# A two-layer hybrid encoder on one core: the q/kv projection group made token-major, and layer 1's modulation and conv taps spread anew

## The chip, the core and the metric

The kernel runs on one core of a Trainium2 chip. The core has five engines with a queue each: PE multiplies matrices, DVE (VectorE) and ACT (ScalarE) do elementwise work, POOL (GpSimd) small work, and SP issues DMA transfers. PE writes only to PSUM (eight banks of 128 x 512 f32), from where DVE or ACT fetch the results. The metric is the device time of one execution in microseconds (us).

## The reference

The input x is 256 tokens by 2048 channels, in f32, and goes through two layers. Each layer normalizes x, scales and shifts it by vectors made from c ("modulation"), projects it with one matrix of 4288 columns, runs four mixers on parts of the columns, projects back, and then does a gated feed-forward part with a width-3 convolution.

```python
c_act = silu(c)
for l in range(2):
    mod = (c_act @ w_mod[l] + b_mod[l]).reshape(bn, 6, d)     # shift, scale, gate for mixing, and again for the FFN
    h = layer_norm(x) * (1.0 + scale_m) + shift_m
    uv, q_c, kv_c, k_r, sb, sc, sh, ag = split(h @ w_in[l])   # widths 1024, 384, 256, 64, 512, 512, 512, 1024
    y_a = gmlp_mixer(uv, ...)        # u * (W_s LN(v) + b), W_s masked: rows 64.. see columns 64.. only
    y_b = mla_mixer(q_c, kv_c, k_r, ...)
    y_c = short_conv_mixer(sb, sc, sh, ...)
    y_d = conformer_conv(ag, ...)    # GLU, depthwise causal conv of 31 taps, layer norm, swish
    y = concatenate([y_a, y_b, y_c, y_d]) @ w_out[l]
    x = layer_norm(ALPHA * x + (1.0 + gate_m) * y) * g + b
    h = layer_norm(x) * (1.0 + scale_f) + shift_f
    x = layer_norm(ALPHA * x + (1.0 + gate_f) * conv_ffn(h, ...)) * g + b

def mla_mixer(q_c, kv_c, k_r, ...):
    q = rms_norm(q_c, q_norm_g) @ w_uq      # rms_norm: x * rsqrt(mean(x^2) + eps) * g
    kv = rms_norm(kv_c, kv_norm_g) @ w_ukv
    k_rope = apply_rope(k_r, cos, sin)
    ...                                     # masked softmax attention, 4 heads
```

The change touches the product that gives q_c, kv_c and k_r (704 columns, group "B" below), the rms_norm behind it, the mask of W_s, and the order of some work.

## The kernel before

**Products.** The input projection is cut into groups of columns: D (ag, 1024), U and V (uv, 512 each), B (q_c, kv_c, k_r, loaded 768 wide), C (sc and sh, 1024) and E (sb, 512). Each group runs over 16 k-tiles of 128 rows of w_in. In layer 1 a weight tile (`wraw`, from DRAM) is split into a rounded part `whi` (ACT, L455) and a rest `wlo` (DVE, L456), both in the reduced type fp32r; the activations are split likewise (`hT`), and each product is made as three fp32r products: hi x hi, hi x rest, rest x hi. The split tiles have four buffers each, the raw ones four in all. In layer 0, groups B and C use exact f32 products instead, with no split (`wexact`, `hF`); an exact product appears in the trace as two records.

`group` computes channel-major results: 128 weight columns are the stationary operand, 256 tokens stream by, and six blocks of 128 columns fill three PSUM banks two by two (`B_c`). All matmuls go through `mm`, so they carry line 79.

**Staging.** `run` goes through the units of a group: `stream` loads a unit, then issues the products of the unit before, then `pump()`s the modulation, then takes up to `bg` pieces off the list of background work. Layer 1's groups come in the order V, D, U, B, C, E, then the output projection ("out").

**Modulation.** The products with w_mod are made on DVE: for each k-tile a 1 MB transfer (`wmod`) and one step over 128 x 2048 elements (`macc`, L233 and L235), sixteen steps for each of the six vectors of a layer. How many steps go with one unit of a group is set by `RATES`.

**Taps.** The 31-tap convolution of group D is made of 124 small operations, 31 for each of four channel blocks: the first of a block is on ACT, the other 30 on DVE (L834). They wait on the background list until the units of U, B, C and E take them (`STEPS` says how many a unit takes).

**The order on an engine.** The program is given in the order in which the functions issue it, and a planner then interleaves it by its own estimates: for instance it puts C products between the steps of `mix_b`, and taps wherever it takes DVE to be free. What comes out is fixed when the program is built: each engine runs its own list in order, and an instruction that waits holds all behind it.

**mix_b** (L950 on) takes group B's result. It squares five of the six blocks on ACT (L968), scales q_c by its gain into `qg` (ACT, L972) and kv_c into `kvr` (DVE, L975), and multiplies the rotary key by cosine and sine into `kc` (DVE, L978 and L979). The mean squares need sums over channels, which lie on partitions, so PE sums them with a column of ones (`ps_ss`); DVE scales them and adds epsilon (L987, L990), POOL raises them to -1/2 (L105), and for kv_c a diagonal matrix and a product with ones (`ps_rkv`) bring the factors to all partitions, where DVE multiplies them in (L1003). The factor of q_c is left to the softmax's scale. Then `ps_kr` (the rotary key), `ps_qn`, `ps_qr`, `ps_kn`, `ps_v`, the scores `ps_sc` and so on.

**mix_v** makes the gated mixer. PE transposes the spatial weights (`ps_wT`), DVE copies them to `wT` (L914), and POOL then writes zeros on the masked block (L915); `ps_mix` on PE reads wT.

Of the kernel before, what the change touches and what calls it, by code (L numbers as in the profile page):

```python
# [7 lines left out]
F32 = mybir.dt.float32  # L8
F32R = mybir.dt.float32r
AF = mybir.ActivationFunctionType  # L10
ALU = mybir.AluOpType
AX = mybir.AxisListType

P = 128
D = 2048
S = 256
DEPTH = 2
W_G = 512
KT = D // P
D_FF = 5632  # L20
NF = D_FF // P
Q_LORA = 384
KV_LORA = 256
HEADS = 4
IN_COLS = 4288
C_UV, C_Q, C_SB, C_SC, C_AG = 0, 1024, 1728, 2240, 3264
ALPHA = (2.0 * DEPTH) ** 0.25
LN_EPS = 1e-5
RMS_EPS = 1e-6
ATT_SCALE = 192.0 ** -0.5  # L30
# [3 lines left out]

RATES = [
    dict(B=1.3, C=1.6, out=2.1, up=0.7, down=0.7),
    dict(D=0.2, U=0.4, V=0.0, B=0.2, C=0.5, E=0.6, out=0.6, up=0.3, down=0.7),
]

STEPS = [  # L40
    dict(B=7, C=8, up=2),
    dict(U=6, B=5, C=6, E=6, up=2),
]

PIECES = ((0, 2), (2, 2), (4, 4), (8, 4), (12, 4))
# [5 lines left out]
def encoder_kernel(ctx: ExitStack, tc: tile.TileContext, A: dict, consts: bass.AP, out: bass.AP):  # L51
# [17 lines left out]
    def tmp_tile(name):  # L69
        return tmpp.tile([P, 512], F32, tag="tmp", name=name)  # L70

    def ms_tile(name):
        return msp.tile([P, 512], F32, tag="ms", name=name)

    def acc_tile(name):
        return accp.tile([P, 512], F32, tag="acc", name=name)

    def mm(o, lhsT, rhs, start, stop):
        pe.matmul(o, lhsT, rhs, start=start, stop=stop, skip_group_check=True)  # L79
# [4 lines left out]
    def slot(name, dtype=F32):  # L84
        return slotp.tile([P, 1024], dtype, tag="slot", name=name)
# [14 lines left out]
    pool.memset(ones, 1.0)  # L100
    mhalf = keep.tile([P, 4], F32, name="mhalf")
    pool.memset(mhalf, -0.5)

    def power(o, i):
        pool.tensor_tensor(out=o, in0=i, in1=mhalf[:, : i.shape[1]], op=ALU.pow)  # L105
# [361 lines left out]
    hT = []  # L467
# [60 lines left out]
    def group2(w, c0, name, then, bg=0, spare=0):  # L528
# [21 lines left out]

        return KT // nk, load, products, lambda: then(box["c"]), bg

    hN, first = [], []

    def first_group(w, c0, then):
# [23 lines left out]
    def run(g):  # L579
        units, load, products, end, bg = g  # L580
        for u in range(units):
            stream(lambda: load(u), lambda item, u=u: products(item, u), bg)
        pending.append(end)
# [223 lines left out]
    def mixers(l, w_in, Y, hF=None, between=None):  # L807
# [91 lines left out]
        def mix_v():  # L899
            ua, va = Y["a"], Y["v"]  # L900
            ga = raw_tile("gmlp")
            nc.sync.dma_start(
                out=ga[:, 0:512].rearrange("p (h j) -> p h j", h=4), in_=A["gmlp_w_s"][l].rearrange("h i j -> i h j")
            )
            nc.sync.dma_start(out=ga[:, 512:1024], in_=A["gmlp_ln_g"][l].partition_broadcast(P))
            nc.sync.dma_start(out=ga[:, 1024:1536], in_=A["gmlp_ln_b"][l].partition_broadcast(P))
            nc.sync.dma_start(
                out=ga[:, 1536:2048], in_=A["gmlp_b_s"][l].rearrange("h i -> (h i)").partition_broadcast(P)
            )
            wT = slot("wT")[:, :512].rearrange("p (h i) -> p h i", h=4)  # L910
            ps = ms_tile("ps_wT")
            for h in range(4):
                pe.transpose(ps[:, h * P : (h + 1) * P], ga[:, h * P : (h + 1) * P], ident)
            dve.tensor_copy(wT, ps.rearrange("p (h i) -> p h i", h=4))  # L914
            pool.memset(wT[64:128, :, 0:64], 0.0)  # L915
            for t in range(2):
                st = smallp.tile([P, 1, 6], F32, tag="stA", name="stA")
                dve.bn_stats(out=st[:, 0, :], in_=va[:, t, :])
                mv, r = rstd_of(st, f"A{t}", False)
                dve.scalar_tensor_tensor(  # L920
                    out=va[:, t, :], in0=va[:, t, :], scalar=mv[:, 0:1], in1=ga[:, 512:1024], op0=ALU.subtract, op1=ALU.mult
                )
                dve.scalar_tensor_tensor(
                    out=va[:, t, :], in0=va[:, t, :], scalar=r[:, 0:1], in1=ga[:, 1024:1536], op0=ALU.mult, op1=ALU.add
                )
            for b in range(2):
                ps = ms_tile("ps_mix")
                for hh in range(2):
                    h = 2 * b + hh
                    for t in range(2):  # L930
                        o = ps[:, hh * S + t * P : hh * S + (t + 1) * P]
                        mm(o, va[:, t, h * P : (h + 1) * P], wT[:, h, :], True, True)
                mixed = tmp_tile("mixed").rearrange("p (h t i) -> p h t i", h=2, t=2)
                bias = ga[:, 1536 + b * S : 1536 + (b + 1) * S].rearrange("p (h i) -> p h i", h=2)
                for t in range(2):
                    dve.tensor_tensor(
                        out=mixed[:, :, t, :],
                        in0=ps.rearrange("p (h t i) -> p h t i", h=2, t=2)[:, :, t, :],
                        in1=bias,
                        op=ALU.add,  # L940
                    )
                dve.tensor_tensor(
                    out=ua[:, 2 * b : 2 * b + 2, :],
                    in0=ua[:, 2 * b : 2 * b + 2, :],
                    in1=mixed.rearrange("p h t i -> p h (t i)"),
                    op=ALU.mult,
                )


        def mix_b(cps, _):  # L950
            wq0, wq1, wkv = raw_tile("wq0"), raw_tile("wq1"), raw_tile("wkv")
            WQ = [wq0[:, 0:768], wq0[:, 768:1536], wq1[:, 0:768]]
            for j in range(3):
# [3 lines left out]
            nc.sync.dma_start(  # L957
                out=wkv.rearrange("p (k c) -> p k c", k=2), in_=A["mla_w_ukv"][l].rearrange("(k p) c -> p k c", p=P)
            )
            qg = slot("qg")[:, :768].rearrange("p (j s) -> p j s", j=3)  # L960
            kvr = slot("kvr")[:, :768].rearrange("p (j s) -> p j s", j=3)
            bank = [(cps[i // 2], (i % 2) * S) for i in range(6)]
            sq = [tmp_tile("sqB0"), tmp_tile("sqB1"), tmp_tile("sqB2")]
            sqs = []
            for i in range(5):
                ps, o = bank[i]
                s = sq[i // 2][:, (i % 2) * S : (i % 2) * S + S]
                act.activation(out=s, in_=ps[:, o : o + S], func=AF.Square)  # L968
                sqs.append(s)
            for j in range(3):  # L970
                ps, o = bank[j]
                act.activation(out=qg[:, j, :], in_=ps[:, o : o + S], func=AF.Copy, scale=QG(j))  # L972
            for j in range(2):
                ps, o = bank[3 + j]
                dve.tensor_scalar(out=kvr[:, j, :], in0=ps[:, o : o + S], scalar1=KVG(j), scalar2=None, op0=ALU.mult)  # L975
            ps, o = bank[5]
            kc, ks = tmp_tile("kc"), None
            dve.tensor_tensor(out=kc[0:64, 0:S], in0=ps[0:64, o : o + S], in1=cosT[0:64, :], op=ALU.mult)  # L978
            dve.tensor_tensor(out=kc[0:64, S : 2 * S], in0=ps[0:64, o : o + S], in1=sinT[0:64, :], op=ALU.mult)  # L979
            ps = ms_tile("ps_ss")  # L980
            for t in range(2):
                for j in range(3):
                    mm(ps[:, t : t + 1], sqs[j][:, t * P : (t + 1) * P], ones[:, 0:1], j == 0, j == 2)
                for j in range(2):
                    mm(ps[:, 2 + t : 3 + t], sqs[3 + j][:, t * P : (t + 1) * P], ones[:, 0:1], j == 0, j == 1)
            rr = smallp.tile([P, 8], F32, tag="rr", name="rr")
            dve.tensor_scalar(  # L987
                out=rr[:, 0:2], in0=ps[:, 0:2], scalar1=1.0 / Q_LORA, scalar2=RMS_EPS, op0=ALU.mult, op1=ALU.add
            )
            dve.tensor_scalar(  # L990
                out=rr[:, 2:4], in0=ps[:, 2:4], scalar1=1.0 / KV_LORA, scalar2=RMS_EPS, op0=ALU.mult, op1=ALU.add
            )
            power(rr[:, 4:8], rr[:, 0:4])
            dve.tensor_scalar(out=rr[:, 4:6], in0=rr[:, 4:6], scalar1=ATT_SCALE, scalar2=None, op0=ALU.mult)
            dg = tmp_tile("dgB")
            for t in range(2):
                dve.tensor_scalar(
                    out=dg[:, t * P : (t + 1) * P], in0=ident, scalar1=rr[:, 6 + t : 7 + t], scalar2=None, op0=ALU.mult
                )
            ps = ms_tile("ps_rkv")  # L1000
            mm(ps[:, :S], ones, dg[:, :S], True, True)
            for j in range(2):
                dve.tensor_tensor(out=kvr[:, j, :], in0=kvr[:, j, :], in1=ps[:, :S], op=ALU.mult)  # L1003

            rope = slot("rope").rearrange("p (j s) -> p j s", j=4)
            ps = ms_tile("ps_kr")
# [157 lines left out]
        phase(l, "U")  # L1164
        run(group(w_in, C_UV, 512, f"U{l}", mix_uv, nk=4, bg=STEPS[l]["U"]))
        phase(l, "B")
        run(group(w_in, C_Q, 768, f"B{l}", mix_b, bg=STEPS[l]["B"]))
        phase(l, "C")
        run(group(w_in, C_SC, 1024, f"C{l}", mix_c, bg=STEPS[l]["C"]))
        phase(l, "E")  # L1170
# [3 lines left out]
    def by_pieces(l, w_in, hF, between, mix_d, mix_u, gelu_v, mix_v, mix_b, mix_c, mix_e):  # L1174
# [93 lines left out]
            gelu_v(t, sums["V"][t])  # L1268
        mix_v()
        phase(l, "B")  # L1270
        run(group(w_in, C_Q, 768, f"B{l}", mix_b, hF=hf, bg=STEPS[l]["B"]))
        phase(l, "C")

        def mix_ce(cps, tps):
# [260 lines left out]
```

## Time and profile before

| | us |
|---|---|
| three runs | 2286.57, 2292.60, 2292.98 (median 2292.6) |
| the profiled execution, its own time | 2285.5 |
| its span, first to last instruction | 2283.7 |
| PE busy | 2226.7 (98%) |
| DVE busy | 1788.8 (78%) |
| ACT busy | 1049.8 (46%) |
| POOL busy | 35.3 (2%) |

All lines below come from the profiled execution. A row of the instructions in order of time gives start, length, engine, line, operation, what it writes from what it reads, shapes and count; in brackets stands the engine's idle time before it and what ended that. A row of grouped instructions has busy time and mean length (ns) after the first bar, and the idle time before the group after the second. A row of the chain of waits has start, length, engine, tile and count.

### The profile page before, as it was taken

Reading aid. Unit: us, or ns where it says so; the run is one execution under the profiler, and the core shown is the slowest. Engines: PE = TensorE matmul, PEld = TensorE weight load, DVE = VectorE, ACT = ScalarE, POOL = GpSimd, SP = SyncE. Lnnn points to the kernel's source line nnn. Section 1 sums busy time; section 2 is a strip of 40 time slices with the busy share of each in tenths; the row PEclk is TensorE's granted clock in tenths of the full one; section 3 lists DMA queues with packets and bytes.
Section 4 is the critical chain, followed back from the end, with each engine's and each line's share of the span. In section 5 each row is a group of like instructions: output and inputs, shape, how many; then the busy total and the mean of one; then the engine's idle time right before and its main releaser. Section 6 shows DMA issues by size and latency. Waiting matters only on the chain. (4 is left out here: it accounts for less than half of the span.)

```text
span 2283.7 us, 30024 instructions
## 1 busy us (share of the span) xinstructions
PE 2226.7 (98%) x11682; PEld 1859.8 (81%) x11682; DVE 1788.8 (78%) x2270; ACT 1049.8 (46%) x1525; POOL 35.3 (2%) x59
## 2 busy tenths in 40 slices
PE   5899999999999999999999999999999999999998
PEld 4688886478888888887887999877888888888886
DVE  6878998598888898998976799787776565665676
ACT  2221141355554544544556434556555554454553
POOL 2000000000000000000000000000000000000000
PEclk9999999999999999999999999999999999999999
DMA  9999889778998988888974666876765556555554
GB/s 348 368 335 342 304 301 393 301 267 304 319 329 302 323 312 327 317 316 304 319 258 148 200 214 240 291 268 223 247 223 190 184 182 199 186 196 190 193 194 147
DMA packets 224566, 605.21 MB, mean 265 GB/s; under 512 B 14548, under 2 KB 27076, under 8 KB 202660
## 3 DMA queue, kind: packets, MB, share of 16 engines
q1 hardware_dynamic: 223576, 602.30, 74.7%
q8 instruction: 91, 1.49, 0.3%
q0 software_dynamic: 848, 1.01, 0.1%
q14 instruction: 51, 0.42, 0.0%
HBM read 601.16 MB, written 2.10 MB: 264 GB/s over the span
## 5 line engine op out<-in xcount | busy, mean ns | idle before, releaser
L456 DVE TENSOR_TENSOR wlo<-wraw,whi 128x1024 fp32r<-128x1024 f32 (+1 forms) x624 | 749.6, 1214 | 315.5 <-ACT whi L455 309.4
L455 ACT CAST whi<-wraw 128x1024 fp32r<-128x1024 f32 (+1 forms) x624 | 649.2, 1047 | 727.2 <-PE g_c L79 204.4
L79 PE MATMUL v_c<-hT,whi 128*128 128x512 f32 x1408 | 493.1, 394 | 0.0
L79 PE MATMUL g_c<-hT,whi 128*128 128x512 f32 x1280 | 448.2, 394 | 0.0
L79 PE MATMUL v_c<-hT,wlo 128*128 128x256 f32 x1408 | 394.3, 280 | 0.0
L79 PE MATMUL d<-whi,a 128*128 128x512 f32 x1344 | 387.9, 390 | 0.0
L235 DVE SCALAR_TENSOR_TENSOR macc<-wmod,cact,macc 128x2048 f32<-128x2048 f32 x150 | 351.6, 2344 | 17.1 <-DMA wmod<-in_w_mod_dram 16.8
L79 PE MATMUL g_c<-hT,wlo 128*128 128x256 f32 x1280 | 358.4, 280 | 0.0
L79 PEld LDWEIGHTS v_c<-hT,whi 128*128 128x128 f32 x1408 | 263.9, 187 | 61.0
L79 PEld LDWEIGHTS d<-whi,a 128*128 128x128 f32 x1344 | 252.9, 188 | 52.4
L79 PEld LDWEIGHTS g_c<-hT,whi 128*128 128x128 f32 x1280 | 239.9, 187 | 55.6
L79 PEld LDWEIGHTS v_c<-hT,wlo 128*128 128x128 f32 x1408 | 265.8, 189 | 0.2
L79 PEld LDWEIGHTS g_c<-hT,wlo 128*128 128x128 f32 x1280 | 241.7, 189 | 0.2
L79 PE MATMUL d<-wlo,a 128*128 128x512 f32 x672 | 233.8, 390 | 1.9 <-DVE wlo L456 1.9
L79 PEld LDWEIGHTS d<-wlo,a 128*128 128x128 f32 x672 | 126.6, 188 | 29.1 <-DVE wlo L456 2.7
L79 PE MATMUL o<-whi,a 128*128 128x512 f32 x352 | 102.3, 398 | 2.3 <-ACT whi L455 2.3
L834 DVE SCALAR_TENSOR_TENSOR convD<-gluD,pm,convD 128x237 f32<-128x237 f32 (+26 forms) x240 | 99.0, 458 | 0.5
L474 ACT CAST a<-g 128x512 fp32r<-128x512 f32 x132 | 81.1, 616 | 36.7 <-PE d L79 34.2
L79 PE MATMUL D_c<-hT,whi 128*128 128x256 f32 x448 | 85.7, 292 | 4.0 <-ACT hT L474 3.0
L475 DVE TENSOR_TENSOR a<-g,a 128x512 fp32r<-128x512 f32 x132 | 87.5, 683 | 1.8 <-ACT a L474 1.8
L566 PE MATMUL first<-wexact,hN 128*128 128x512 f32 x192 | 85.7, 596 | 1.5 <-ACT hN L82 1.2
L235 DVE SCALAR_TENSOR_TENSOR qacc<-wmod,cact,qacc 128x1024 f32<-128x1024 f32 (+1 forms) x75 | 80.2, 1070 | 2.4 <-DMA wmod<-in_w_mod_dram 0.4
(311 smaller groups left out, 2462.3 us busy)
## 6 DMA issues: line engine op xcount, KB each, us to landing
wraw<-in_ffn_w_up_dram SPq DMA_DIRECT2D x168, 1024.0 KB, 5.2
wmod<-in_w_mod_dram SPq DMA_DIRECT2D x160, 1024.0 KB, 6.6
wraw<-in_ffn_w_down_dram SPq DMA_DIRECT2D x88, 1024.0 KB, 5.3
wmod<-in_w_mod_dram SPq DMA_DIRECT2D x64, 512.0 KB, 7.9
wraw<-in_w_in_dram SPq DMA_DIRECT2D x30, 1024.0 KB, 5.5
wexact<-in_w_in_dram SPq DMA_DIRECT2D x52, 512.0 KB, 6.7
wraw<-in_w_out_dram SPq DMA_DIRECT2D x24, 1024.0 KB, 7.3
wexact<-in_w_out_dram SPq DMA_DIRECT2D x16, 512.0 KB, 11.0
```

The costliest lines, as they stand in the source:

```text
L79: pe.matmul(o, lhsT, rhs, start=start, stop=stop, skip_group_check=True)
L235: i = dve.scalar_tensor_tensor(out=acc, in0=w, scalar=col, in1=acc, op0=ALU.mult, op1=ALU.add)
L455: held(act.copy(hi[:, :m], r), "cast")
L456: i = dve.tensor_tensor(out=lo[:, :m], in0=r, in1=hi[:, :m].bitcast(F32), op=ALU.subtract)
L474: act.copy(hi, src)
L475: dve.tensor_tensor(out=lo, in0=src, in1=hi.bitcast(F32), op=ALU.subtract)
L566: i = pe.matmul(ps, hN[kt // 4][:, kt % 4, t * P : (t + 1) * P], parts[kt], start=kt == 0, stop=kt == KT - 1, skip_group_check=True,)
L834: dve.scalar_tensor_tensor(out=yd[:, j, 30 - k :], in0=glu[:, j, : S - 30 + k], scalar=CW(k, j), in1=yd[:, j, 30 - k :], op0=ALU.mult, op1 ...
```

## The change

Four edits stand together.

**Group B becomes token-major.** A new `latent_group` takes the place of `group` for B in both layers. The activations of 128 tokens are the stationary operand and the weight columns stream by: for each k-tile, token tile and term one product of 512 columns into a bank of its own (`B_w`) and one of 192 columns into half of a shared bank (`B_n`). 704 columns are loaded in place of 768.

**mix_b works on rows of tokens.** The squares are taken by ACT with an accumulated sum along the row, so PE's sums, the diagonal matrix and the broadcast go; POOL adds the two parts of kv_c's sum, adds epsilon and takes the power, ATT_SCALE being put into the constants. ACT copies q_c and the rotary key, and copies kv_c scaled by its factor; twelve transposes on PE then turn these to channel-major, where gains and cosines are applied as before.

**RATES and STEPS of layer 1.** More modulation steps with D and E's units, none with U's, B's and C's; taps per unit 7, 4, 4 and 8 for U, B, C and E.

**wT.** The zeros are written ahead of the transposes, and DVE copies only the rest, in two pieces.

```diff
 RATES = [
     dict(B=1.3, C=1.6, out=2.1, up=0.7, down=0.7),
-    dict(D=0.2, U=0.4, V=0.0, B=0.2, C=0.5, E=0.6, out=0.6, up=0.3, down=0.7),
+    dict(D=1.0, U=0.0, V=0.0, B=0.0, C=0.0, E=0.9, out=0.6, up=0.3, down=0.7),
 ]
 STEPS = [
     dict(B=7, C=8, up=2),
-    dict(U=6, B=5, C=6, E=6, up=2),
+    dict(U=7, B=4, C=4, E=8, up=2),
 ]
+    rms_eps = keep.tile([P, 4], F32, name="rms_eps")
+    pool.memset(rms_eps[:, 0:2], RMS_EPS / ATT_SCALE**2)
+    pool.memset(rms_eps[:, 2:4], RMS_EPS)
+    def latent_group(w, c0, name, then, hF=None, bg=0):
+        nk = 2
+        box = {}
+        def products(item, u):
+            if u == 0:
+                box["wide"] = [acc_tile(f"{name}_w{t}") for t in range(2)]
+                both = acc_tile(f"{name}_n")
+                box["narrow"] = [both[:, t * 192 : (t + 1) * 192] for t in range(2)]
+                box["h"] = list(hT)
+            for k, (hi, lo) in enumerate(item):
+                kt = u * nk + k
+                st, sp = kt == 0, kt == KT - 1
+                for t in range(2):
+                    tok = slice(t * P, (t + 1) * P)
+                    outs = ((box["wide"][t], slice(0, 512), st), (box["narrow"][t], slice(512, 704), st and t == 0))
+                    if lo is None:
+                        for o, c, first in outs:
+                            mm(o, hF(kt)[:, tok], hi[:, c], first, sp)
+                        continue
+                    xh, xl = (h[:, kt % 2, tok] for h in box["h"][kt // 2][:2])
+                    for o, c, first in outs:
+                        mm(o, xh, hi[:, c], first, False)
+                    for o, c, _ in outs:
+                        mm(o, xh, lo[:, c], False, False)
+                    for o, c, _ in outs:
+                        mm(o, xl, hi[:, c], False, sp)
+        def load(u):
+            return weights(w, u * nk, nk, c0, 704, hF is not None)
+        return KT // nk, load, products, lambda: then(box["wide"], box["narrow"]), bg
...
+            pool.memset(wT[64:128, :, 0:64], 0.0)
             ps = ms_tile("ps_wT")
...
-            dve.tensor_copy(wT, ps.rearrange("p (h i) -> p h i", h=4))
-            pool.memset(wT[64:128, :, 0:64], 0.0)
+            by_head = ps.rearrange("p (h i) -> p h i", h=4)
+            dve.tensor_copy(wT[0:64], by_head[0:64])
+            dve.tensor_copy(wT[64:128, :, 64:128], by_head[64:128, :, 64:128])
...
-        def mix_b(cps, _):
+        def mix_b(wide, narrow):
...
+            lat = [tmp_tile("lat0"), tmp_tile("lat1"), tmp_tile("lat2")]
+            rest = [lat[2][:, t * 192 : (t + 1) * 192] for t in range(2)]
+            ss = smallp.tile([P, 8], F32, tag="rr", name="ss")
+            for t in range(2):
+                for at, junk, ps, n in (
+                    (0, lat[t][:, 0:384], wide[t][:, 0:384], Q_LORA * ATT_SCALE**2),
+                    (2, lat[t][:, 384:512], wide[t][:, 384:512], KV_LORA),
+                    (4, rest[t][:, 0:128], narrow[t][:, 0:128], KV_LORA),
+                ):
+                    act.activation(
+                        out=junk, in_=ps, func=AF.Square, scale=float(n) ** -0.5, accum_out=ss[:, at + t : at + t + 1]
+                    )
+                act.copy(lat[t][:, 0:384], wide[t][:, 0:384])
+                act.copy(rest[t][:, 128:192], narrow[t][:, 128:192])
+            rr = smallp.tile([P, 8], F32, tag="rr", name="rr")
+            pool.tensor_tensor(out=ss[:, 2:4], in0=ss[:, 2:4], in1=ss[:, 4:6], op=ALU.add)
+            pool.tensor_tensor(out=rr[:, 0:4], in0=ss[:, 0:4], in1=rms_eps, op=ALU.add)
+            power(rr[:, 4:8], rr[:, 0:4])
+            for t in range(2):
+                for o, ps in ((lat[t][:, 384:512], wide[t][:, 384:512]), (rest[t][:, 0:128], narrow[t][:, 0:128])):
+                    act.activation(out=o, in_=ps, func=AF.Copy, scale=rr[:, 6 + t : 7 + t])
...
+            def turn(ps, o, parts):
+                for t in range(2):
+                    n = parts[t].shape[1]
+                    pe.transpose(ps[0:n, o + t * P : o + (t + 1) * P], parts[t], ident)
+                return ps[:, o : o + S]
+            ps = ms_tile("ps_q")
+            for j in range(2):
+                by = turn(ps, j * S, [lat[t][:, j * P : (j + 1) * P] for t in range(2)])
+                act.activation(out=qg[:, j, :], in_=by, func=AF.Copy, scale=QG(j))
...
+            ps = ms_tile("ps_kv")
+            for j in range(2):
+                by = turn(ps, j * S, [lat[t][:, 384:512] if j == 0 else rest[t][:, 0:128] for t in range(2)])
+                dve.tensor_scalar(out=kvr[:, j, :], in0=by, scalar1=KVG(j), scalar2=None, op0=ALU.mult)
...
-        run(group(w_in, C_Q, 768, f"B{l}", mix_b, bg=STEPS[l]["B"]))
+        run(latent_group(w_in, C_Q, f"B{l}", mix_b, bg=STEPS[l]["B"]))
...
-        run(group(w_in, C_Q, 768, f"B{l}", mix_b, hF=hf, bg=STEPS[l]["B"]))
+        run(latent_group(w_in, C_Q, f"B{l}", mix_b, hF=hf, bg=STEPS[l]["B"]))
```

More of the change, by code (lines that the diff above doesn't have):

```diff
@@ L960, in mix_b @@
             qg = slot("qg")[:, :768].rearrange("p (j s) -> p j s", j=3)
             kvr = slot("kvr")[:, :768].rearrange("p (j s) -> p j s", j=3)
[L962 to L969, printed above, removed]
@@ L970, in mix_b @@
-            for j in range(3):
-                ps, o = bank[j]
-                act.activation(out=qg[:, j, :], in_=ps[:, o : o + S], func=AF.Copy, scale=QG(j))
-            for j in range(2):
[L974 to L1001, printed above, removed]
+            def turn(ps, o, parts):
[3 more added lines that the diff above has]
+                return ps[:, o : o + S]
@@ new lines, in mix_b @@
+            ps = ms_tile("ps_q")
+            for j in range(2):
+                by = turn(ps, j * S, [lat[t][:, j * P : (j + 1) * P] for t in range(2)])
+                act.activation(out=qg[:, j, :], in_=by, func=AF.Copy, scale=QG(j))
+            ps = ms_tile("ps_q")
+            by = turn(ps, 0, [lat[t][:, 256:384] for t in range(2)])
+            act.activation(out=qg[:, 2, :], in_=by, func=AF.Copy, scale=QG(2))
+            by = turn(ps, S, [rest[t][:, 128:192] for t in range(2)])
+            kc = tmp_tile("kc")
@@ L1002, in mix_b @@
+            dve.tensor_tensor(out=kc[0:64, 0:S], in0=by[0:64, :], in1=cosT[0:64, :], op=ALU.mult)
+            dve.tensor_tensor(out=kc[0:64, S : 2 * S], in0=by[0:64, :], in1=sinT[0:64, :], op=ALU.mult)
+            ps = ms_tile("ps_kv")
             for j in range(2):
-                dve.tensor_tensor(out=kvr[:, j, :], in0=kvr[:, j, :], in1=ps[:, :S], op=ALU.mult)
+                by = turn(ps, j * S, [lat[t][:, 384:512] if j == 0 else rest[t][:, 0:128] for t in range(2)])
+                dve.tensor_scalar(out=kvr[:, j, :], in0=by, scalar1=KVG(j), scalar2=None, op0=ALU.mult)
```

## The prediction

> **What bounds the kernel now.** I read the page's first part, then busy time by stage, then the instructions in order of time around the q/kv group ("B"). The stages below are layer 1's D, U, B, C and E groups and layer 0's B, C and output projection; times are us, the second column PE's busy time.
>
> ```profile
> PE 2226.7 (98%) x11682; PEld 1859.8 (81%) x11682; DVE 1788.8 (78%) x2270; ACT 1049.8 (46%) x1525; POOL 35.3 (2%) x59
> core 0: us, PE busy (x) PEld busy (x) DVE busy (x) ACT busy (x) POOL busy (x), PEclk, DMA share, GB/s
> 1230.10:1276.10 46.00, 46.00 (x386) 46.00 (x385) 24.28 (x21) 16.75 (x17) 0.55 (x1) 1.00 0.70 241
> 1276.10:1299.30 23.20, 23.20 (x196) 23.20 (x195) 20.84 (x32) 13.48 (x18) 0.00 (x0) 1.00 0.50 164
> 1299.30:1338.00 38.70, 36.89 (x310) 36.68 (x308) 38.53 (x74) 15.92 (x25) 0.86 (x3) 1.00 0.68 212
> 1338.00:1413.20 75.20, 75.05 (x534) 69.74 (x535) 67.23 (x122) 29.58 (x48) 1.12 (x1) 1.00 0.71 248
> 1413.20:1440.80 27.60, 27.33 (x220) 26.83 (x219) 24.36 (x36) 16.74 (x24) 1.08 (x1) 1.00 0.54 190
> 189.90:233.40 43.50, 43.50 (x212) 38.31 (x211) 42.05 (x82) 9.37 (x19) 2.83 (x5) 1.00 0.92 324
> 233.40:325.50 92.10, 91.98 (x442) 76.97 (x440) 85.53 (x143) 22.71 (x43) 3.69 (x2) 1.00 0.86 315
> 345.00:425.00 80.00, 76.89 (x244) 44.83 (x243) 61.59 (x48) 9.86 (x15) 0.00 (x0) 0.96 1.01 396
> ```
>
> PE is busy nearly without a gap where the change acts: the span moves by PE's work and by gaps in it. Layer 1's B stage is the tight one: DVE is busy 38.53 of 38.70 us, so any DVE work added there ends last. In layer 0, DVE (42.05 of 43.50) and the DMA engines (1.01 at 345 to 425) are nearly full too.
>
> **Prices on PE.** Matmuls overlap, so I take spacings: length of a run over its count.
>
> ```profile
> 2032.91 239.69 PE d L79 x1056
> 1608.86 22.19 PE v_c L79 x128
> 1552.20 11.16 PE first L566 x26
> 1534.61 0.44 PE ps_xT L612 x4
> 203.07 30.38 PE L79 MATMUL B_c<-hF,wexact 128*128 128x256 f32 x140
> ```
>
> fp32r, 512 columns: 239.69/1056 = 0.227 us. v_c is 64 pairs of 512 and 256 columns: 22.19/64 = 0.347, so 256 columns cost 0.120. An f32 product is two records: 0.429 each at 512 columns (11.16/26), 0.216 at 256 (30.22/140). A transpose: 0.11.
>
> **The layer 1 B group.** It had 288 products of 256 columns: 34.6 us. Now 96 of 512 and 96 of 192. The wide ones: 96 x 0.227 = 21.8 us. No fp32r product in this trace is narrower than 256, so 192 has to be bounded: from below by columns, 0.120 - 64 x (0.227 - 0.120)/256 = 0.093; from above by f32, two records of 0.216 x 192/256, 0.325. The group takes 30.7 to 53.0 us. The nearest row by type is 0.120 (33.3 us), nearer the lower end. I still take the upper end, and say why after the DVE queue; the choice costs 20 us on PE.
>
> The Trainium skill, "TensorE: Matmul & The Clock Gate" (LDWEIGHTS (loading the stationary operand); Back-to-back issue gap) says loading 128 weight columns takes 128/1.2 = 107 ns and a warm product N/2.4 + 2.5 ns; 192 columns would then cost 107 ns, bound by the load, and the group 32 us by that estimate. For 256 the page gives 109 ns against 120 here, and f32's 0.216 is its value for twice the columns; no run here shows 192. It speaks for the rival below.
>
> **DVE in that stage.** Queues run in order, so the built order decides. First the prices (start to next start), among them the transposed spatial weights wT that PE's ps_mix waits for:
>
> ```profile
> 1277.48 2.35 DVE L235 SCALAR_TENSOR_TENSOR macc<-wmod,cact,macc 128x2048 f32<-128x2048 f32 x1 [0.59 <-DMA wmod<-in_w_mod_dram]
> 1279.75 1.28 DVE L823 TENSOR_TENSOR gluD<-D_c,sg 128x512 f32<-128x512 f32 x2
> ...
> 1302.28 0.67 DVE L914 COPY wT<-ps_wT 128x512 f32<-128x512 f32 x1
> ...
> 1305.27 0.40 DVE L936 TENSOR_TENSOR mixed<-ps_mix,gmlp 128x256 f32<-128x256 f32 x1
> 1305.60 0.44 DVE L834 SCALAR_TENSOR_TENSOR convD<-gluD,pm,convD 128x235 f32<-128x235 f32 x1
> ...
> 1306.68 0.67 DVE L942 TENSOR_TENSOR ya<-ya,mixed 128x512 f32<-128x512 f32 x1
> 1307.28 0.44 DVE L834 SCALAR_TENSOR_TENSOR convD<-gluD,pm,convD 128x233 f32<-128x233 f32 x1
> ...
> 1310.90 0.94 DVE L456 TENSOR_TENSOR wlo<-wraw,whi 128x768 fp32r<-128x768 f32 x1
> 1311.77 1.20 DVE L834 SCALAR_TENSOR_TENSOR convD<-gluD,pm,convD 128x229 f32<-128x229 f32 x3
> 1312.89 0.94 DVE L456 TENSOR_TENSOR wlo<-wraw,whi 128x768 fp32r<-128x768 f32 x1
> ...
> 1334.42 1.21 DVE L456 TENSOR_TENSOR wlo<-wraw,whi 128x1024 fp32r<-128x1024 f32 x1
> 1335.56 0.44 DVE L834 SCALAR_TENSOR_TENSOR convD<-gluD,pm,convD 128x231 f32<-128x231 f32 x1
> ```
>
> A tap is 0.38; a split of 768 columns 0.87, so 704 about 0.80; one of 1024 1.14; "mixed" 0.33, "ya" 0.60. Before, 48 taps stood between wT and the rotary key products kc. In the changed program all 91 taps still left stand there, seven or so ahead of each split that PE needs; none is left for C and E. From wT to the last of the group's 13 remaining splits: 73 taps (27.7), 13 splits (10.4), mixed 1.3, ya 1.2, two more splits "a" of ya (as ya, 1.2): 41.8 us.
>
> PE needs a split after two products of each k-tile, so it cannot run ahead. wT was copied at 1302.28. Now six more taps stand ahead of the copy (+2.3) and the copy is two with a tap between (+0.7); the GLU starts some 2 us earlier, since no modulation step stands just before it any more (that at 1277.48 held it until 1279.75). I leave the end of the copies at 1303, near where PE resumed before, within 1 us:
>
> ```profile
> 1299.34 0.48 PE L79 MATMUL B_c<-hT,whi 128*128 128x256 f32 x2
> 1303.42 2.05 PE L79 MATMUL ps_mix<-wT,va 128*128 128x128 f32 x16 [1.81 <-POOL wT L915]
> 1337.70 0.28 PE L79 MATMUL B_c<-hT,wlo 128*128 128x256 f32 x1
> 1337.82 0.95 PE L79 MATMUL ps_ss<-ones,sqB 128*128 128x1 f32 x8
> 1345.00 1.13 PE L79 MATMUL ps_kr<-kc,cst 64*128 64x256 f32 x4
> ```
>
> So the zeroed block written first buys nothing: the memset leaves the chain, one tap and a second copy take its place. Last split at 1303 + 41.8 = 1344.8, ten products behind it (1.6 to 2.8 us): by DVE the group ends at 1346.5. By PE, at the upper price: 1299.34 + 53.0 + 2.05 for ps_mix + 1 idle = 1355.4. It ended at 1337.98. **Plus 8.5 us by DVE alone, plus 17.4 if 192 columns go at f32's price.** The two overlap: the later end counts. Why I take the second: so much filler among so few splits is the layout for a group well over 40 us. That is no time, only a hint at which end fits, and it is why this case gets little over half.
>
> **From the group's end to ps_kr.** Before 7.0 us, all PE work: sums of squares, C products, the broadcast. Now PE has ten transposes (1.1) and 35 C products (4.2), 5.3 us, behind a chain on ACT and POOL.
>
> ```profile
> L968 ACT ACTIVATE sqB<-B_c 128x256 f32<-128x256 f32 x10 | 3.5, 393 | 25.9 <-PE B_c L79 25.9
> L1082 ACT ACTIVATION_READ_ACCUMULATOR p<-ps_sc,sm,rr 128x1 f32 x16 | 3.1, 196 | 0.0
> 236.19 2.34 DVE L235 SCALAR_TENSOR_TENSOR macc<-wmod,cact,macc 128x2048 f32<-128x2048 f32 x1
> 236.41 2.99 POOL L105 TENSOR_TENSOR rr<-rr,mhalf 128x4 f32<-128x4 f32 x1 [32.40 <-DVE rr L990]
> 1341.47 1.12 POOL L105 TENSOR_TENSOR rr<-rr,mhalf 128x4 f32<-128x4 f32 x1 [37.49 <-DVE rr L990]
> ```
>
> Six squares at 0.39 + 0.20 and four copies at about 0.4 are 5.1 us of ACT; the first token tile is ready 1.7 us before the end, so the last square ends near +2.6. POOL's two adds have no row: between nothing and the power's 1.12; I take 0.7 each, so the factors stand at +5.1, three scaled copies make it +6.3, and ps_kr comes at about +7: no change (bounds -1.7 and, with every POOL step at 2.99, +6). If DVE is the late one, kc follows 18 taps and two splits (9.1 us) after the last split, at 1353.9, and ps_kr at about 1354.6: +9.6. The skill's "SBUF — State Buffer" (the shared port pair) says a GpSimd operation and a VectorE one with two SBUF inputs lock each other out for a whole instruction: 2.99 beside a 2.34 us step against 1.12 agrees. By it each of the three could wait for a split of 1.14, and the sum would gain 2.8.
>
> Softmax cover in C shrinks from 76 to 45 products (5.4 us) before the first transposes; the chain there (table load, four exponentials, scaling) is about as long: +0.5. The modulation's steps only move. Eight of 2.35 stand in D now (three before): 18.8 us of DVE beside 16 splits (18.2) in 46 us. SP issues each step's 1 MB between two of D's weight loads, from the same four raw buffers; 5 MB more in 46 us lift 241 to some 350 GB/s, below the 396 seen. So D costs nothing as long as each lands in time (rival 3). POOL's two new memsets at the start and its rope memsets, now behind the power, cost nothing: it is busy 35.3 us in all, and rope is wanted after ps_kr.
>
> **Layer 0.** 96 f32 products x 2 x 0.216 = 41.5 us become 32 x 2 x 0.429 + 32 x 2 x 0.162 = 37.8: -3.7. Sums and broadcast give way to transposes: -1.3. The chain costs 1.8 (power at 1.1) to 3.7 (2.99) of PE's idle time. DVE sheds about 1 us and is full until 325, and the output projection waits for DMA, so what PE gains may be lost there: -3.5 to 0; I take -2.
>
> **Sum**, against the profiled run's own 2285.5 (span 2283.7, 1.8 around it): 17.4 + 0 + 0.5 - 2 = +15.9, 2301.4. The three runs had a median of 2292.6, 7.1 above that execution, and one at 2286.6; I add half of the 7.1: 2305.
>
> **The rivals.** (1) 192 columns cost 0.093 to 0.12 and DVE sets the group: +9.6 + 0.5 - 2 = +8.1, 2293.6, with 3.5 more 2297. For it: the price by type. Against: the layout. 0.27. (2) Faster: the saving on PE counts in full, -3.9 in layer 1's group, -3.7 in layer 0's, -1.3 in each for the sums, -10 in all, 2275.3 (2279 with the 3.5). It needs DVE to hold no split back, so taps at 0.2 in place of 0.38, or another order. 0.08. (3) D starves: a split stands behind a step whose wmod is late, for eight units at up to 1 us: +16 + 8, 2309.5 (2313). 241 GB/s becoming 350 speaks for it, the 396 against. It decides from 0.7 us a unit on. 0.07. (4) No change that shows: rival 1 with layer 0's full gain and short waits, +5 or less, 2290. 0.06. The forecast itself has 0.52.
>
> **Numbers.** Within 0.3% (6.9 us) a measurement here cannot tell a change from none. Slower: 0.52 + 0.27 + 0.07; faster 0.08; same 0.06. Range: rival 1 at its least, 2291, to the forecast with a median high as before's, no gain in layer 0 and POOL waits, 2301.4 + 7.1 + 2 + 4 = about 2315. The forecast's own is 2299 to 2315.
>
> **What would show it.** B_n spaced at 0.3 us; layer 1's B from first to last product at 56 us (47 for rival 1, with PE idle behind wlo); no tap after kc; layer 0's B near 40. Wrong if PE's gaps in layer 1's B are under 5 us in all and B_n costs 0.12 or less.

## The result and the profile after

| | before | changed |
|---|---|---|
| median of six runs, us | 2290.47 | 2304.65 |
| lowest to highest, us | 2283.04 to 2292.98 | 2299.77 to 2309.53 |
| ratio to before | | 1.0066, 95% interval 1.0045 to 1.0088 |
| profiled execution: time, span, us | 2285.5, 2283.7 | 2301.89, 2300.1 |

The change makes the kernel 0.66% slower. The forecast was 2305, by 17.4 us more in layer 1's B group and little elsewhere. The time is right; half of the way to it is not, as the stages show. First the profile's own sum of busy time by engine, of the changed kernel:

```profile
PE 2221.2 (97%) x11502; PEld 1839.0 (80%) x11502; DVE 1785.8 (78%) x2258; ACT 1055.2 (46%) x1555; POOL 38.9 (2%) x65
```

PE does 5.5 us less work than before (2226.7) and the span is 16.4 us longer: the time is in gaps and in clock, not in products. Busy time by stage of the changed kernel says where; the stages are layer 1's D group, its B group, B's end to `ps_kr`, the rest of C, and layer 0's B group (stretch, its length, busy time of PE, PEld, DVE, ACT, POOL, granted PE clock, DMA share, GB/s):

```profile
1230.00:1276.90 46.90, 46.90 (x387) 46.42 (x386) 37.23 (x30) 16.80 (x18) 2.11 (x3) 1.00 1.00 362
1300.30:1347.20 46.90, 37.22 (x211) 30.48 (x209) 46.66 (x106) 14.78 (x24) 0.00 (x0) 1.00 0.40 113
1347.20:1359.70 12.50, 6.14 (x45) 5.35 (x45) 9.81 (x19) 5.62 (x21) 2.59 (x5) 1.00 0.44 158
1359.70:1429.90 70.20, 70.11 (x480) 64.89 (x480) 32.37 (x51) 27.93 (x45) 0.00 (x0) 0.98 0.52 174
189.90:233.60 43.70, 41.62 (x147) 25.25 (x145) 40.33 (x74) 8.24 (x17) 1.92 (x2) 0.96 0.84 290
```

Against before: layer 1's B took 38.7 us and takes 46.9 (+8.2), with DVE busy in 46.66 of them and PE in 37.22; B's end to `ps_kr` took 7.0 and takes 12.5 (+5.5); the rest of C took 68.2 (1345.0 to 1413.2) and takes 70.2 (+2.0). With the 1.0 us by which B starts later, that is 16.7 of the 16.4 us; the rest of the program gives 0.3 back.

**B's products are cheap.** PE's instructions in order of time, at the group's start and near its end:

```profile
1300.32 0.47 PE L79 MATMUL B_w<-whi,hT 128*128 128x512 f32 x1
1300.63 0.25 PE L79 MATMUL B_n<-whi,hT 128*128 128x192 f32 x1
1300.72 0.41 PE L79 MATMUL B_w<-wlo,hT 128*128 128x512 f32 x1
...
1303.21 0.46 PE L79 MATMUL ps_mix<-wT,va 128*128 128x128 f32 x2 [1.04 <-DVE wT L956]
...
1340.65 0.25 PE L79 MATMUL B_n<-whi,hT 128*128 128x192 f32 x1
1342.03 0.50 PE L79 MATMUL B_w<-wlo,hT 128*128 128x512 f32 x1 [1.13 <-DVE wlo L461]
1342.37 0.25 PE L79 MATMUL B_n<-wlo,hT 128*128 128x192 f32 x1
1342.46 0.41 PE L79 MATMUL B_w<-whi,hT 128*128 128x512 f32 x1
```

From a narrow product's start to the next start is 0.09 us (1300.63 to 1300.72, 1342.37 to 1342.46): the lower bound of the prediction, not the 0.325 it took. A wide and a narrow one take about 0.34 together, the group's 96 pairs 32.6 us, which is less than the 34.6 it had. PE then stands idle in front of each `wlo`. DVE's list shows why (same view, DVE):

```profile
1337.66 0.88 DVE L461 TENSOR_TENSOR wlo<-wraw,whi 128x704 fp32r<-128x704 f32 x1
1338.46 2.71 DVE L873 SCALAR_TENSOR_TENSOR convD<-gluD,pm,convD 128x229 f32<-128x229 f32 x7
1341.09 0.88 DVE L461 TENSOR_TENSOR wlo<-wraw,whi 128x704 fp32r<-128x704 f32 x1
...
1349.09 2.45 DVE L873 SCALAR_TENSOR_TENSOR convD<-gluD,pm,convD 128x237 f32<-128x237 f32 x5
1351.46 1.22 DVE L461 TENSOR_TENSOR wlo<-wraw,whi 128x1024 fp32r<-128x1024 f32 x1
```

One split and seven taps are 3.43 us (1337.66 to 1341.09); a k-tile's six pairs cost PE 2.04.

**A late load behind the same taps.** Three of the four raw buffers hold `wq0`, `wq1` and `wkv` by then, so C's weights go through the last one, which the split at 1351.46 frees. Rows of the same view, of SP's queue of DMA issues (SPq), DVE, ACT and PE:

```profile
1352.71 9.40 SPq L446 DMA_DIRECT2D wraw<-in_w_in_dram  x2
```

```profile
1355.92 0.41 DVE L1043 TENSOR_TENSOR kc<-ps_q,cst 64x256 f32<-64x256 f32 x1
```

```profile
1357.89 1.04 ACT L460 CAST whi<-wraw 128x1024 fp32r<-128x1024 f32 x1 [5.05 <-DMA wraw<-in_w_in_dram]
1358.84 0.47 ACT L1037 ACTIVATE qg<-ps_q,pm 128x256 f32<-128x256 f32 x1
```

```profile
1359.36 0.44 PE L1031 MATMUL ps_kv<-cst,lat 128*128 128x128 f32 x2 [3.42 <-ACT qg L1037]
1359.73 0.48 PE L79 MATMUL ps_kr<-kc,cst 64*128 64x256 f32 x1
```

The load is issued 0.03 us after the split ends, and the cast that waits for it starts 5.2 us later, when `kc` has long been made. `qg` stands behind the cast in ACT's list, `ps_kv` needs its bank emptied by `qg`, and `ps_kr` stands behind `ps_kv`. C's own next products need the same cast, which ends at 1358.93. Behind that gap PE's clock falls, in the stretches by time (PE's busy time, clock, DMA share, GB/s); the last row is layer 0's B, behind a gap of 2.08 us at 200.4:

```profile
1360.00:1362.00 2.00, 2.00 (x9) 0.66 0.00 0
1362.00:1364.00 2.00, 2.00 (x8) 0.50 0.62 104
...
200.00:210.00 10.00, 7.92 (x32) 0.83 0.53 180
```

If the time lost is a stretch's length times what its clock lacks of 1.00, that is (0.34 + 0.50) x 2 = 1.7 us in layer 1, nearly all of the 2.0 that C's rest grew by.

### The profile page after: what moved, and what is told of

Read it like the earlier page. It is cut to its first block, busy times and chain, and to the rows that moved or that the text cites. A ratio compares the mean times of both kernels' runs of the same rounds, so it can differ in the third digit from the quotient of the medians.

```text
span 2300.1 us, 29686 instructions
## 1 busy us (share of the span) xinstructions
PE 2221.2 (97%) x11502; PEld 1839.0 (80%) x11502; DVE 1785.8 (78%) x2258; ACT 1055.2 (46%) x1555; POOL 38.9 (2%) x65
## 5 line engine op out<-in xcount | busy, mean ns | idle before, releaser
L873 DVE SCALAR_TENSOR_TENSOR convD<-gluD,pm,convD 128x249 f32<-128x249 f32 (+26 forms) x240 | 98.6, 458 | 0.7
L479 ACT CAST a<-g 128x512 fp32r<-128x512 f32 x132 | 81.1, 616 | 35.8 <-PE d L79 32.6
```

What stands on the lines that cost most here:

```text
L479: act.copy(hi, src)
L873: dve.scalar_tensor_tensor(out=yd[:, j, 30 - k :], in0=glu[:, j, : S - 30 + k], scalar=CW(k, j), in1=yd[:, j, 30 - k :], op0=ALU.mult, op1 ...
```

## The experiments

Three theories stood. **Order**: the products are cheap; the taps ahead of the splits and what follows from them cost the time, and they stand there because the narrow product is 192 wide (the planner's own estimate makes such products long, it seems, and fills DVE to match). **Product**: the token-major form and its chain cost it, wherever the taps are. **Rates**: the moved modulation costs it. Ratios are to the runs of the kernel before in the same comparison, whose medians were 2287.4, 2288.4 and 2287.3 in the three comparisons below (four, three and two kernels).

**1. The narrow product padded to 256 columns, in layer 1 alone.** More work, other order.

```diff
+        width = 704 if hF is not None else 768
...
-                    outs = ((box["wide"][t], slice(0, 512), st), (box["narrow"][t], slice(512, 704), st and t == 0))
+                    outs = (
+                        (box["wide"][t], slice(0, 512), st),
+                        (box["narrow"][t][:, 0 : width - 512], slice(512, width), st and t == 0),
+                    )
...
-            return weights(w, u * nk, nk, c0, 704, hF is not None)
+            return weights(w, u * nk, nk, c0, width, hF is not None)
```

> The changed kernel, but in layer 1 the narrow product is 256 columns wide in place of 192 (the group is loaded 768 wide again, the last 64 columns are not used). PE gets more work: 64 columns x 96 products, about 2.6 us by the spacings 0.120 and 0.093. In the built order 58 taps stand between wT and kc in place of 92, and 44 come after it in place of 8. Order theory (the taps ahead of the splits, put there because of the width 192, cost the time, and the products themselves are cheap): the B group of layer 1 ends PE-bound, 36 to 39 us after its first product in place of 46.9, and the kernel is 6 to 12 us faster than the changed one, 1 to 8 us slower than before. Product theory (the token-major form and its chain through ACT and POOL cost the time, wherever the taps stand): 2 to 3 us slower than the changed kernel, 16 to 17 us slower than before.

Measured: 2291.8, ratio 1.0012 (1.0001 to 1.0024): by the ratios 12 us faster than the changed kernel. (The traces have 36 taps behind `kc` here and none in the changed kernel; the 44 and 8 above take in eight later steps on the same tile.) Its stages (columns as above: layer 1's B, B's end to `ps_kr`, rest of C):

```profile
1303.50:1339.80 36.30, 36.18 (x212) 31.41 (x210) 36.05 (x73) 15.53 (x24) 0.00 (x0) 1.00 0.61 182
1339.80:1350.30 10.50, 6.92 (x46) 6.15 (x44) 6.05 (x14) 6.04 (x21) 4.47 (x5) 0.86 0.22 88
1350.30:1419.60 69.30, 68.87 (x481) 63.84 (x481) 47.26 (x88) 27.35 (x45) 0.00 (x0) 1.00 0.53 177
```

With 64 columns more in each narrow product the group is 10.6 us shorter than the changed one's, and PE is busy in all of it: that is order, not product. Product theory is out as the account of these 12 us. What it says of the chain behind B is not: B's end to `ps_kr` takes 10.5 us here, 7.0 before.

**2. 448 + 256 columns in place of 512 + 192, in layer 1.** No column added.

```diff
+        cut = 512 if hF is not None else 448
...
-                    outs = ((box["wide"][t], slice(0, 512), st), (box["narrow"][t], slice(512, 704), st and t == 0))
+                    outs = (
+                        (box["wide"][t][:, 0:cut], slice(0, cut), st),
+                        (box["narrow"][t][:, 0 : 704 - cut], slice(cut, 704), st and t == 0),
+                    )
...
```

> The changed kernel, but in layer 1 the 704 columns are cut 448 + 256 in place of 512 + 192, with no column added; one more scaled copy on ACT for each token tile. 54 taps stand between wT and kc, 46 after it. Order theory: as with the padded product, less about 2 us of PE: 8 to 14 us faster than the changed kernel, 1 us faster to 6 us slower than before. Product theory: same time as the changed kernel, 13 to 16 us slower than before.

Measured: 2291.53, ratio 1.0014 (1.0001 to 1.0027).

```profile
1301.90:1335.10 33.20, 33.03 (x213) 31.33 (x211) 33.11 (x68) 14.68 (x23) 0.00 (x0) 1.00 0.63 187
1335.10:1346.90 11.80, 7.30 (x49) 6.78 (x48) 7.02 (x17) 6.46 (x23) 5.32 (x5) 0.86 0.26 89
```

B is now 33.2 us, 5.5 less than before the change. Of these, 3.9 are PE's work (36.89 to 33.03 us busy) and 1.6 the wait for wT, which is 0.17 us here: the token-major form does save PE work. But the whole is no faster than before, since 11.8 us lie between B and `ps_kr` where there were 7.0, with PE idle in 4.5.

**3. The changed kernel with the old rates.**

```diff
-    dict(D=1.0, U=0.0, V=0.0, B=0.0, C=0.0, E=0.9, out=0.6, up=0.3, down=0.7),
+    dict(D=0.2, U=0.4, V=0.0, B=0.2, C=0.5, E=0.6, out=0.6, up=0.3, down=0.7),
-    dict(U=7, B=4, C=4, E=8, up=2),
+    dict(U=6, B=5, C=6, E=6, up=2),
```

> The changed kernel with layer 1's rates of the modulation and taps per unit as before. In the built order 96 taps stand between wT and kc. Order theory: no better than the changed kernel, 12 to 18 us slower than before, since the taps follow from the width and not from the rates. Rates theory (the moved modulation and the new taps per unit cost the time): within 3 us of before.

Measured: 2311.3, ratio 1.0092 (1.0075 to 1.0108): slower still, by the ratio 21 us behind before, where order theory had 12 to 18. B takes 49.4 us with DVE busy in 48.8, and `ps_kr` waits 6.2 us for `kc`. Rates theory is out.

**4. The new rates alone, on the kernel before** (the same lines the other way round).

> The kernel before with only layer 1's rates of the modulation and taps per unit as in the changed kernel. 52 taps stand between wT and kc (48 before). Order theory: within 4 us of before, either way. Rates theory: 10 to 16 us slower than before.

Measured: 2291.7, ratio 1.0015 (1.0000 to 1.0029): some 3 us slower, with anything from nothing to 6.6 us inside the interval, and in any case under the 10 of rates theory. B takes 37.1 us, and from its end to `ps_kr` it is:

```profile
1333.30:1340.50 7.20, 7.20 (x49) 6.87 (x47) 3.72 (x13) 2.51 (x4) 1.10 (x1) 0.76 0.37 139
```

PE is busy in all of these 7.2 us, but its clock is 0.76: 1.7 us lost, and behind no gap. The last section comes back to it.

So order theory stands for B, and a second loss is left: PE idle behind B. Rows of the cut 448 + 256 in order of time, POOL, then DVE, then ACT, then PE (`ss` are the sums of squares, `rr` the factors made from them, `lat` the rows copied for the transposes):

```profile
1336.80 3.49 POOL L1023 TENSOR_TENSOR ss<-ss 128x2 f32<-128x2 f32 x1 [96.59 <-ACT lat L1017]
1340.37 0.20 POOL L1024 TENSOR_TENSOR rr<-ss,rms_eps 128x4 f32<-128x4 f32 x1
1340.64 1.01 POOL L110 TENSOR_TENSOR rr<-rr,mhalf 128x4 f32<-128x4 f32 x1
```

```profile
1334.04 6.20 DVE L877 SCALAR_TENSOR_TENSOR convD<-gluD,pm,convD 128x228 f32<-128x228 f32 x16
```

```profile
1341.69 0.31 ACT L1031 ACTIVATE lat<-B_w,rr 128x64 f32<-128x64 f32 x1 [4.55 <-POOL rr L110]
...
1343.00 0.51 ACT L1046 ACTIVATE qg<-ps_q,pm 128x256 f32<-128x256 f32 x1
```

```profile
1343.56 0.69 PE L1040 MATMUL ps_q<-cst,lat 128*128 128x128 f32 x2 [4.50 <-ACT qg L1046]
```

POOL's add of two numbers per row takes 3.49 us, and ends at 1340.29, just after DVE's run of 16 taps (1334.04 + 6.20 = 1340.24). The next add takes 0.20. ACT's scaled copies wait for POOL; `qg`, which needs nothing of POOL, waits behind them; PE waits for `qg`. Two theories: **POOL** (this wait, passed on by ACT's list) and **ACT** (the squares and copies themselves are long).

**5. The kv factor late.** The scaled copies, `ps_kv` and `kvr` are issued just ahead of `ps_kn`, in both layers; no line changes but its place.

```diff
+            for t in range(2):
...
+                for o, ps in parts:
+                    act.activation(out=o, in_=ps, func=AF.Copy, scale=rr[:, 6 + t : 7 + t])
+            ps = ms_tile("ps_kv")
...
```

> As the cut 448 + 256, and in both layers the part of mix_b that needs the root mean square of kv_c (the scaled copies on ACT, the transposes ps_kv and kvr) is issued after the rotary query, just ahead of ps_kn, instead of ahead of qg's second half. Nothing is added or removed. POOL theory (PE's idle 4.5 us in layer 1 and 3.8 in layer 0 behind mix_b come from POOL's first add, which ends only when DVE's run of taps ends, and ACT's in-order queue passes that on to qg; the lowered clock behind each gap follows from the gap): both gaps shrink below 1 us, the clock behind them stays at 1.0, and the kernel is 6 to 12 us faster than with the cut alone, 2 to 8 us faster than before. ACT theory (the chain of squares and copies itself is long): no more than 2 us faster than with the cut alone.

Measured: 2288.43, ratio 1.0000 (0.9989 to 1.0012). A miss: some 3 us better than the cut (the two intervals overlap), where POOL theory had 6 to 12. The edit did not do what was meant, so it decides between neither theory. ACT's rows of this kernel:

```profile
1338.26 0.31 ACT L1080 ACTIVATE lat<-B_w,rr 128x64 f32<-128x64 f32 x1 [3.43 <-POOL rr L110]
1338.47 0.31 ACT L1080 ACTIVATE lat<-B_n,rr 128x64 f32<-128x64 f32 x1
1338.67 0.47 ACT L1038 ACTIVATE qg<-ps_q,pm 128x256 f32<-128x256 f32 x1
```

The planner had put two scaled copies ahead of `qg` all the same, and the gap at `ps_q` stayed at 3.4 us.

**6. Layer 0 channel-major again, layer 1 cut 448 + 256.**

```diff
-            return by_pieces(l, w_in, hF, between, mix_d, mix_u, gelu_v, mix_v, mix_b, mix_c, mix_e)
+            return by_pieces(l, w_in, hF, between, mix_d, mix_u, gelu_v, mix_v, mix_b_old, mix_c, mix_e)
...
-        run(latent_group(w_in, C_Q, f"B{l}", mix_b, hF=hf, bg=STEPS[l]["B"]))
+        run(group(w_in, C_Q, 768, f"B{l}", mix_b, hF=hf, bg=STEPS[l]["B"]))
```

> As the cut 448 + 256 in layer 1, but layer 0 has the channel-major group and the mix_b of before. If what layer 0 loses behind its group B (4.6 us at the end of C in the profiled execution) lasts to the end: 3 to 5 us faster than with the cut alone. If it is taken up by the stages behind it: within 2 us of the cut alone.

Measured: 2287.37, ratio 0.9996 (0.9985 to 1.0007). Against the cut's 1.0014 that is 4 us, but the two intervals overlap: likely, not certain.

**7. The wT edit alone, on the kernel before.**

> The kernel before with only the wT edit (zeros written ahead of the transposes, DVE's copy in two pieces). By the prediction the edit buys nothing: within 2 us of before, and ps_mix in layer 1 comes within 1 us of where it came. If POOL's write behind the copy was worth its 1.8 us of PE's idle time: 1 to 3 us faster.

Measured: 2288.99, ratio 1.0002 (0.9992 to 1.0011). `ps_mix` in layer 1 waited 1.81 us for POOL before; here it waits 2.14 for DVE's copy. The edit buys nothing.

**8. The scaled copies on DVE**, on top of the late kv factor: now ACT's list cannot hold `qg` behind POOL.

```diff
-    act.activation(out=o, in_=ps, func=AF.Copy, scale=rr[:, 6 + t : 7 + t])
+    dve.tensor_scalar(out=o, in0=ps, scalar1=rr[:, 6 + t : 7 + t], scalar2=None, op0=ALU.mult)
```

> As the run with the kv factor late, but the scaled copies of kv_c are made by DVE in place of ACT. In that run the built order had still put two scaled copies ahead of qg on ACT, so the gap stayed (3.4 us in layer 1, 3.7 in layer 0). Now ACT's list has none, and on DVE they stand behind 9 taps (13 before) and ahead of kc. POOL theory (PE's gap is ACT's queue waiting for POOL): no gap at ps_q in either layer; what is left is a shorter one at ps_kr, under 2 us, since kc waits for the factors; 2 to 6 us faster than with the cut alone. ACT theory (squares and copies are the long part): the gap at ps_q stays over 2 us and the time within 2 us of the cut alone.

Measured: 2280.85, ratio 0.9966 (0.9955 to 0.9977): by the ratios 11 us faster than the cut alone, where 2 to 6 were expected, and by the medians 6.5 us faster than before. Its stages, as above, then POOL's and DVE's rows:

```profile
1298.60:1331.60 33.00, 32.81 (x211) 31.09 (x209) 32.91 (x68) 14.46 (x23) 0.00 (x0) 1.00 0.64 188
1331.60:1337.30 5.70, 4.70 (x38) 4.18 (x36) 4.24 (x14) 4.72 (x17) 2.61 (x5) 1.00 0.56 184
```

```profile
1333.50 0.78 POOL L1023 TENSOR_TENSOR ss<-ss 128x2 f32<-128x2 f32 x1 [96.63 <-ACT lat L1017]
```

```profile
1330.72 3.50 DVE L877 SCALAR_TENSOR_TENSOR convD<-gluD,pm,convD 128x228 f32<-128x228 f32 x9
1335.69 0.28 DVE L1080 TENSOR_SCALAR lat<-B_w,rr 128x64 f32<-128x64 f32 x1 [1.46 <-POOL rr L110]
```

From B's end to `ps_kr` are 5.7 us in place of 11.8, at full clock. ACT's squares and the copies that stay with it are as before, so the ACT theory is out. `qg` starts on ACT at 1334.14, before POOL's first add has ended: it no longer waits for POOL. The run of taps ahead of the waiting copies is 9 long now, it ends at 1334.22, and POOL's add ends at 1334.28: with the run, the wait shrank too, as POOL theory has it. In the cut's profile PE's gaps behind the two B groups (4.50 and 4.36 us) and the clock behind them (1.7 and 3.4) make 14.0 us; here the gaps are 1.00 and 1.73 and the clock loses 1.7 in layer 0 alone, 4.4 in all. The difference of 9.6 is close to the 11 measured; the expected 2 to 6 is no more than the gaps alone, 6.1 us less here.

**9. The same with layer 0 channel-major** (the edits of 6 and 8).

> As the run before it, but layer 0 has the channel-major group and the mix_b of before. Layer 0's part: the channel-major layer 0 made the cut alone 4 us faster (ratio 0.9996 against 1.0014). If that was PE's gap behind layer 0's B, and DVE's copies have removed it, this run is within 2 us of the one before it; if it was something else in layer 0, 3 to 4 us faster. By the best sum 3 to 6 us faster than the kernel before.

Measured: 2280.71, ratio 0.9970 (0.9959 to 0.9981), the same as the eighth. So the 4 us of the sixth, if they are real, fit PE's gap behind layer 0's B, and the token-major form of layer 0 shows neither a cost nor a gain beyond that, as far as these intervals tell (3 to 4 us). The eighth, which keeps the token-major group in both layers, and this one are the fastest here.

## Why the prediction came out right, and where it did not

- **What bounds the kernel**: right. DVE's list sets layer 1's B, and the taps in it move the end.
- **Price of 192 columns: the failed step.** "If 192 columns go at f32's price" (0.325 us) was taken, for 17.4 us. Measured is 0.09, the lower bound of 0.093. The reason given, that so much filler fits a long group, read the built order as evidence of the chip. It tells at most what the planner reckons: in experiment 1 a wider product drew fewer taps ahead of `kc` (58 for 92) and a shorter group. The planner's own price was not read, only inferred from that. The row nearest by type, 256 columns at 0.120, had the answer, and the Trainium skill, "TensorE: Matmul & The Clock Gate" (LDWEIGHTS (loading the stationary operand); Back-to-back issue gap), spoke for it: the estimate of 32 us for the group by its figures stands beside the measured 32.6, though the single narrow product, at 0.09 us from start to start, lies under the 107 ns that the Trainium skill gives a load of 128 columns.
- **DVE's queue in B**: right to within 0.3 us. By DVE the group was to end 8.5 us later; it takes 8.2 more, and the last product starts at 1346.88 with the start 1.0 late. The end of wT's copies was put at 1303; `ps_mix` starts at 1303.21. That is rival 1's mechanism, which had 0.27. So are the signs: 46.9 us for B (47 named for rival 1, 56 for the forecast), PE idle behind `wlo`, narrow products 0.09 apart and not 0.3.
- **B's end to `ps_kr`**: 0 was taken, 5.5 measured, inside the bounds of -1.7 and +6. Neither POOL nor `kc` set it in the changed kernel: `kc` starts at 1355.92 (forecast 1353.9 where DVE is late), but a weight load freed late by a split came in between. The prediction counted what waits for a split on PE and forgot that a split also frees the buffer of the next load. POOL's three steps, taken at 2.5 us, took 2.0 (0.44, 0.30, 1.24); the 2.8 named for waits of three splits does not follow from three times 1.14, which is 3.4, but stood in no sum.
- **Clock**: no term for it. 1.7 us behind the gap in layer 1. Softmax's cover was given 0.5; C's rest leaves 0.3 for it.
- **Layer 0**: -2 forecast. B did its products in 3.6 us less PE time, by length less the gap and the lost clock (43.7 - 2.1 - 1.7 against 43.5), but lost it at once: 2.08 us where `ps_mix` waited, since DVE's copy of wT and the layer norm of v behind it came after a step that waited 2.54 us for its wmod, and the clock's 1.7. Then POOL's add took 2.93 us, PE waited 3.82, and the clock behind that lost another 1.7 (0.77, 0.50 and 0.88 in three stretches of 2 us). C ended 4.6 us later than before; of that, 1.0 was left when layer 1's D began, and as much when its B did. Where the other 3.6 went, in stages where PE is busy throughout, is not settled; single executions of one kernel differ by more.
- **The sum**: 9.2 too much for the products, 5.5 + 1.5 + 3.0 too little for the chain, the clock and layer 0. The errors cancel, and the median's 2304.65 beside 2305 is luck to that extent. Rival 1's 2297 had the mechanism of B and missed what follows B.
- **The other rivals**: D did not starve (PE busy 46.90 of 46.90 at 362 GB/s, forecast 350): from its first product to U's first are 46.47 us in both kernels (1229.47 to 1275.94, 1230.46 to 1276.93). PE's saving in full, -10, is what the eighth run comes near to once the waits are gone (some 8 us by the ratio), but by the ninth no part of it that shows comes from layer 0, where the rival had half.

## What to carry to other kernels

When a list built by a planner looks odd around one operation, ask whether the planner's price for it is the chip's (here it was only inferred that it is not); a width that changes the price can move other work more than the operation itself is worth, and padding it is a cheap test. Where an engine's list is the bound, follow each late instruction to all that it frees, loads included, and not only to the one that reads it. A small result of a slow side engine should not stand in a list ahead of work that does not need it: issuing a few small copies later and moving them to another engine was worth 11 us here, some 8 of them from the move.

## What the runs showed of the hardware

In four places POOL's small add met an unbroken run of taps on DVE, each with two SBUF inputs, and ended not with one tap but with the whole run. The run's end and the add's end were 1340.24 and 1340.29 in the second run, 1336.79 and 1336.85 in the fifth, 1334.22 and 1334.28 in the eighth, and in the changed kernel's layer 0:

```profile
231.71 6.47 DVE L873 SCALAR_TENSOR_TENSOR convD<-gluD,pm,convD 128x230 f32<-128x230 f32 x17
```

```profile
235.31 2.93 POOL L1017 TENSOR_TENSOR ss<-ss 128x2 f32<-128x2 f32 x1 [31.76 <-ACT lat L1011]
```

238.18 and 238.24. The Trainium skill, "SBUF — State Buffer" (Terms, "shared port pair"), has the pair of ports that the two engines share locked for one full instruction; here 17 taps of 0.38 us in a row held POOL's add up, so by the measurement the wait can be that of the whole run. In the changed kernel's layer 1, though, an add asked during a split ended with that split, and the next ran beside taps in 0.30 us (POOL, then DVE); what lets POOL in between is open:

```profile
1348.79 0.44 POOL L1017 TENSOR_TENSOR ss<-ss 128x2 f32<-128x2 f32 x1 [110.16 <-ACT lat L1011]
1349.31 0.30 POOL L1018 TENSOR_TENSOR rr<-ss,rms_eps 128x4 f32<-128x4 f32 x1
```

```profile
1347.96 1.22 DVE L461 TENSOR_TENSOR wlo<-wraw,whi 128x1024 fp32r<-128x1024 f32 x1
```

The clock fell behind some gaps and not behind others of the same length. A gap of 1.73 us (layer 0, the eighth run: 0.83 over 6 us and 0.92 over the next 8) and one of 2.08 lost 1.7 us, one of 3.39 in the fifth run lost 3.4; one of 1.81 in the kernel before and one of 2.14 in the padded run kept 1.00. The gaps of about 1.1 us in the changed kernel's layer 1 B, with PE busy in 37.2 of 46.9 us, cost no clock at all. A gap is not needed either: in the fourth run the clock was 0.76 over 7.2 us in which PE was never idle. What it did there, from 1333.19 on, was 20 products of a single column (`ps_ss`) between those of C; the same products in the kernel before kept 1.00 (1338.00 to 1345.00). What decides is open.
